# Where the tiles of a matmul stand in SBUF: the rooms in a fixed order, and one column of padding between the tiles of one of them

## The chip, the cores and the metric

The kernel runs on one core of one Trainium2 chip. The metric is the device time of one execution in microseconds (us); the time before is the median of three executions. Durations inside an execution come from one profiled execution of the same program.

## What is computed

A decoder trunk of two layers over 1024 tokens of width 1024, in float32. Each layer is a norm, one input projection, a retention group and a differential attention group, an output projection, and a gated feed-forward part:

```python
for l in range(DEPTH):
    u = rmsnorm(h, attn_norm[l])
    rq, rk, rv, rg, dq, dk, dv = split(u @ w_in[l])
    ret = silu(rg) * rmsnorm(retention_chunkwise(rq, rk, rv), ret_norm[l])
    dif = rmsnorm(diff_attention(dq, dk, dv, lam), diff_norm[l]) * (1.0 - lam_init)
    h = h + concat([ret, dif]) @ w_out[l]
    u = rmsnorm(h, ffn_norm[l])
    h = h + (silu(u @ w_gate[l]) * (u @ w_up[l])) @ w_down[l]
return rmsnorm(h, final_norm)
```

FFN_HIDDEN is 2816, that is 22 tiles of 128.

## The kernel before, in words

**A product in three matmuls.** A float32 product is made of operands of type float32r, which TensorE streams in one pass. Each operand is kept as two tiles: a rounded one (hi) and what the rounding lost (lo). `mm3` and `product` issue three matmuls for each piece of 128 in the contracted dimension: weights hi with data hi, weights hi with data lo, weights lo with data hi (L246 to L248 and L270 to L272). The weights are the stationary operand, 128x128, of which each matmul loads its own copy; the data is the moving operand, mostly 128x512. In a profile row such as `ps_mm<-u,w` the moving operand stands first after the arrow and the stationary one second. In `tm_pair` (L305 to L307) the roles are turned: tiles of `w` move, 256 columns at a time, and those of `u` are stationary.

**Rooms.** SBUF is shared out by tags, each with a fixed number of rooms that its tiles use in turn. `a4` (8 rooms), `wr` (3), `sp`, `ka`, `v`, `mx` (4 each) and `kb` (2) hold 1024 float32 in each partition, 4096 bytes; `w` (12), `t2` (5) and `acc` (2) hold 512, 2048 bytes; `nx`, `ny` (2 each), `z` and `m` (4 each) hold four numbers, 16 bytes, and each takes 32. `u` has 4 rooms of eight tiles with 512 columns, 16384 bytes. A tag's rooms are laid out, one behind the other, where the program first asks for that tag, so that the order in SBUF is the order of first use.

**Where they stand.** The constants end at byte 5472, which is 96 modulo 256. Every big room is a multiple of 256 bytes long, so that offsets modulo 256 change only at small pieces. In the kernel before the order is `a4`, `wr`, `sp`, `acc`, `kb` (all of them at 96 modulo 256), then `nx` and `ny` (4 x 32 = 128 bytes), then `u`, `t2`, `w`, `mx`, `ka`, `v` (all of them at 96 + 128 = 224 modulo 256). Tiles inside a room begin at multiples of 512 bytes, so the same holds for every tile and every 128-column slice of weights. Below, the *offset* of a matmul is the address of its moving tile less the address of the weights that are loaded while it runs, those of the matmul behind it, modulo 256. Before, it is 0 for data in `u`, `ka`, `v` with weights in `w` or `mx`, and 128 for data in `sp` with weights in `w`, for data in `u` with weights in `kb`, and for `ka` with `a4`.

**Who uses u.** `norm_half` writes the normed activations into two rooms of `u`, one for hi and one for lo, tile k of each for piece k (L421 to L432). `retention` writes the concatenated output there. In the feed-forward part seven data factors stand in rooms named by `TAGS7 = ["u", "u", "ka", "v", "u", "u", "sp"]`, four in `u`, one each in `ka`, `v` and `sp` (`views`); a factor in `u` uses one room, tiles 0 to 3 for hi and 4 to 7 for lo. The last six hidden tiles (`TAILS`) come through `layer`, and some of them also stand in `u`.

**Order of the work.** TensorE's order is written out by hand. In attention its projections are woven with score, transpose and value matmuls (`weave`); in the feed-forward part it runs long rows of 84 matmuls of 128x512 per hidden tile. ScalarE, VectorE and GpSimd make the hi and lo tiles, SyncE issues the DMAs.

Of the kernel before, what the change touches and what calls it, by code (L numbers as in the profile page):

```python
# [12 lines left out]
F32 = mybir.dt.float32  # L13
R32 = mybir.dt.float32r
# [4 lines left out]
P = 128  # L19
D = 1024  # L20
T = 1024
KT = D // P
NH = 2
HT = T // NH
# [5 lines left out]
FAST = 16  # L30
TAILS = [2, 4]
TAGS7 = ["u", "u", "ka", "v", "u", "u", "sp"]
RAWS = ["wr", "wr", "wr", "kb", "kb"]
EPS = 1e-6
NEG = -3.0e38
# [83 lines left out]
class Line:  # L119


    def __init__(self):
        self.n, self.tasks, self.products, self.w, self.made = -1, {}, [], {}, 0
# [23 lines left out]
class Trunk:  # L147
    def __init__(self, tc, ctx, a):
        self.tc, self.nc, self.a = tc, tc.nc, a
        pool = lambda name, **kw: ctx.enter_context(tc.tile_pool(name=name, bufs=1, **kw))  # L150
        self.sb = pool("sb")
        self.ps = pool("ps", space=bass.MemoryType.PSUM)
        self.dr = pool("dr", space=bass.MemoryType.DRAM)
        self.n = 0
        self.wi = 0
        self.consts()


    def t(self, tag, bufs, shape, dt=F32):
# [2 lines left out]

    def big(self, tag, dt=F32):
        return self.t(tag, {"a4": 8, "ka": 4, "kb": 2, "v": 4, "sp": 4, "mx": 4, "wr": 3}[tag], [P, 1024], dt)

    def tmp(self, dt=F32):
        return self.t("t2", 5, [P, 512], dt)
# [58 lines left out]
    def views(self, tag):  # L226

        if tag == "u":
            t = self.t("u", 4, [P, KT, HT], R32)
            return [(t[:, i], t[:, 4 + i]) for i in range(4)]  # L230
        t = [self.big(tag, R32) for _ in range(4)]
        c = [slice(0, 512), slice(512, 1024)]
        return [(t[i // 2][:, c[i % 2]], t[2 + i // 2][:, c[i % 2]]) for i in range(4)]
# [184 lines left out]
    def norm_half(self, h, hf, gcol, us, lag=11, gap=9, first=False, keep=False):  # L418
        nc = self.nc
        sl = slice(hf * HT, hf * HT + HT)  # L420
        parts = self.squares(h, sl, 0, True, first)  # L421
        yield lag
        y = yield from self.rsqrt_rows(parts, D, gap=gap)
        hi = self.t("u", 4, [P, KT, HT], R32)
        lo = self.t("u", 4, [P, KT, HT], R32)
        for k in range(KT):
            f = self.tmp()
            nc.vector.scalar_tensor_tensor(out=f, in0=h[k][:, sl], scalar=self.gains[:, gcol + k:gcol + k + 1],
                                           in1=y, op0=ALU.mult, op1=ALU.mult)
            nc.scalar.copy(hi[:, k], f)  # L430
            eng = nc.gpsimd if keep and k in (1, 4) else nc.vector
            eng.tensor_tensor(out=lo[:, k], in0=f, in1=hi[:, k].bitcast(F32), op=ALU.subtract)  # L432
        if keep:
            self.first_y = self.big("sp")[:, 0:HT]
            nc.scalar.copy(self.first_y, y)
        us[hf] = (hi, lo)
# [13 lines left out]
    def seven_second(self, h, gcol, b, keep, line):  # L450

        nc = self.nc
        v = nc.vector.tensor_tensor
        sl = slice(HT, T)
        parts = self.squares(h, sl, 0)
        yield 15
        y = yield from self.rsqrt_rows(parts, D, gap=9)
        own = self.t("u", 4, [P, KT, HT])
        t22, t12 = [own[:, i] for i in range(4)], [own[:, 4 + i] for i in range(4)]
        c = [slice(0, 512), slice(512, 1024)]  # L460
        b11, b21 = [keep[i // 2][:, c[i % 2]] for i in range(4)], [keep[2 + i // 2][:, c[i % 2]] for i in range(4)]
        b += [self.views(TAGS7[2]), self.views(TAGS7[3]), None, self.views(TAGS7[5]), None]
        two = [self.big("sp") for _ in range(2)]
        t2 = [two[i // 2][:, c[i % 2]] for i in range(4)]

        def norm(f, k):
            nc.vector.scalar_tensor_tensor(out=f, in0=h[k][:, sl], scalar=self.gains[:, gcol + k:gcol + k + 1],
                                           in1=y, op0=ALU.mult, op1=ALU.mult)

        def sub(out, x, z, q=None, i=0):  # L470
            v(out=out, in0=x, in1=z, op=ALU.subtract)
            if q is not None:
                nc.scalar.copy(b[q][i][0], out)

        def low(src, dst):
            v(out=dst[1], in0=src, in1=dst[0].bitcast(F32), op=ALU.subtract)
        r = range(4)
        ops = [lambda i=i: norm(t12[i], i) for i in r]
        ops += [lambda i=i: norm(t22[i], 4 + i) for i in r]
        for i in r:  # L480
            ops.append(lambda i=i: sub(b11[i], t12[i], b11[i]))
            ops.append(lambda i=i: sub(t2[i], t22[i], b11[i], 2, i))
        ops += [lambda i=i: low(t2[i], b[2][i]) for i in r]
        ops += [lambda i=i: self.part(b11[i], b[3][i], nc.vector) for i in r]

        def room(q):
            b[q] = self.views(TAGS7[q])
        ops += [lambda i=i: sub(b11[i], t22[i], t12[i]) for i in r]
        ops += [lambda i=i: self.part(t22[i], b[5][i], nc.vector) for i in r]
        ops.append(lambda: room(4))  # L490
        ops += [lambda i=i: self.part(b11[i], b[4][i], nc.vector) for i in r]
        ops += [lambda i=i: sub(b21[i], b21[i], t2[i]) for i in r]
        ops.append(lambda: room(6))
        ops += [lambda i=i: self.part(b21[i], b[6][i], nc.vector) for i in r]
        for i, op in enumerate(ops):
            line.later(line.n + (i // 3 if i < 21 else 7 + (i - 21) // 6 if i < 37 else 13), op)
# [558 lines left out]
    def right_factors(self, line, fast, m0):  # L1055
# [14 lines left out]
        def one(q, i):  # L1070
            if not b[q]:
                b[q] += self.views(TAGS7[q])
            self.part(stage[q, i - i % 2][:, 512 * (i % 2):512 * (i % 2) + 512], b[q][i],
# [9 lines left out]
    def down_fast(self, line, h, at, f0, b, m):  # L1083
# [3 lines left out]
        for e in range(2):  # L1087
            self.factors(line, at + 2 * e, {j: n0 + 2 * j + e for j in range(7)}, None,
                         [RAWS[(m + e) % 5], RAWS[(m + 2 + e) % 5]],
                         [n for n in range(n0, n0 + 14) if n % 3 == 0])  # L1090
# [25 lines left out]
    def layer(self, l, h, us, w_first, norm1, after):  # L1116
        nc, a = self.nc, self.a
# [5 lines left out]
                nc.sync.dma_start(src[k], h[k])  # L1123
        o_out, rq, rk = self.attention(l, us, w_first, norm1)
        x = self.retention_inputs(us, rq, rk, self.att_close(l))
        mix = [(self.t("u", 4, [P, KT, HT], R32), self.t("u", 4, [P, KT, HT], R32)) for _ in range(NH)]
        for hf in range(NH):
            for hd in range(4):
                s = o_out[hd][:, hf * HT:hf * HT + HT]
                hi, lo = mix[hf]  # L1130
# [6 lines left out]
        rhs = lambda k, hf: (mix[hf][0][:, k], mix[hf][1][:, k])  # L1137
        ws = [self.weight("w" if i < 3 else "kb") for i in range(4)]
        keep = [self.big("mx") for _ in range(4)]
        b = [self.views(tag) for tag in TAGS7[:2]]  # L1140
        self.two_halves(h, 4, ws, rhs, ["mm"], self.seven_first(h, 16 + 8 * l, b, keep))
# [5 lines left out]
        for ci, n in enumerate(TAILS):  # L1147
            acts = []
            for i in range(n):
                if n == 2 or i == 3:  # L1150
                    if n == 4 or i == 0:
                        room = self.t("u", 4, [P, KT, HT], R32).rearrange("p (a k) c -> p a (k c)", a=4)
                    j = 2 * (i % 2) if n == 2 else 0
                    acts.append((room[:, j], room[:, j + 1]))
                else:
                    tag = ["ka", "v", "sp"][i]
                    acts.append((self.big(tag, R32), self.big(tag, R32)))
                s = self.big("mx")
                nc.sync.dma_start(s, rest[t0 + i])
                for hf in range(NH):  # L1160
                    sl = slice(HT * hf, HT * hf + HT)
                    self.part(s[:, sl], [x[:, sl] for x in acts[i]], nc.vector if hf else nc.gpsimd)
            t0 += n
            rhs = lambda k, hf: (acts[k][0][:, hf * HT:hf * HT + HT], acts[k][1][:, hf * HT:hf * HT + HT])
            per = KT // n
            if ci + 1 < len(TAILS):
                for i in range(n):
                    w = self.weight()
                    for hf in range(NH):
                        for f in range(per * i, per * i + per):  # L1170
                            self.drain(self.down_group(h, w, f, hf, n, rhs, "t"))
            else:
                self.exp_ln_set()
                ws = [self.weight("w" if i else "mx") for i in range(4)]
                self.two_halves(h, n, ws, rhs, ["t", "mm"], *after(h))
                return h
# [95 lines left out]
```

## Time and profile before

| | us |
|---|---|
| median of three executions | 2296.06 (2294.91 to 2296.53) |
| the profiled execution: its own time | 2295.52 |
| its span, first to last instruction | 2293.7 |
| TensorE matmuls busy | 2258.2 (98%) |
| TensorE weight loads busy | 1895.4 (83%) |
| VectorE busy | 1396.5 (61%) |
| ScalarE busy | 1009.0 (44%) |
| GpSimd busy | 730.7 (32%) |

The profiled execution is 0.54 us under the median and 1.8 us over its own span. Matmuls overlap: the next one starts while the last results of the one before are still on the way. A row's duration is therefore longer than what the matmul costs in a stream, and the cost is read from the distance between two starts, called the *gap* below. The granted clock of the execution is 0.996 of full speed.

### The profile page before, as it was taken

To read this page: it belongs to the slowest core of one execution; us is meant where nothing else is said; L and a number is where in the kernel's file an instruction comes from. 1 tells how busy PE (TensorE), PEld (TensorE's weight loads), DVE (VectorE), ACT (ScalarE), POOL (GpSimd) and SP (SyncE) were. 2 spreads that over 40 slices of the span, in tenths; PEclk is the share of its full clock that TensorE was granted. 3 is DMA by queue.
4 is the path that set the end of the run, shared out by engine and by line. 5 is a ranking of instruction groups with operands and counts; after the bars stand their busy time and mean duration, and the time that the engine had idled before them with its cause. 6 is when DMAs were issued, how large, how long until landed. Compare 5 with 4: busy or idle time off the path is not lost.

```text
span 2293.7 us, 30632 instructions
## 1 busy us (share of the span) xinstructions
PE 2258.2 (98%) x11328; PEld 1895.4 (83%) x11328; DVE 1396.5 (61%) x2596; ACT 1009.0 (44%) x1905; POOL 730.7 (32%) x588
## 2 busy tenths in 40 slices
PE   7999999999999999999999999999999999999998
PEld 5888898887888888888888888988878888888887
DVE  8777612989544333895567775059884434359856
ACT  5666533445333333543256665234453333344332
POOL 3111212120455455336121112211205445544350
PEclk9999999999999999999999999999999999999999
DMA  4312131112333332652232222112123232346422
GB/s 162 81 47 65 39 97 40 55 56 63 135 106 99 108 106 91 231 183 93 68 108 56 55 66 81 58 38 74 48 96 120 91 116 91 109 150 200 158 65 74
DMA packets 74214, 216.58 MB, mean 94 GB/s; under 512 B 8016, under 2 KB 10064, under 8 KB 74064
## 3 DMA queue, kind: packets, MB, share of 16 engines
q1 hardware_dynamic: 74064, 214.62, 28.9%
q8 instruction: 89, 1.46, 0.3%
q14 instruction: 61, 0.50, 0.1%
HBM read 162.16 MB, written 44.04 MB: 90 GB/s over the span
## 4 chain that ended last, share of the span: by engine, by line
PE 84%; DVE 11%; ACT 2%; issue 1%; DMA 1%; POOL 0%; DVEq 0%; SPq 0%; ACTq 0%; POOLq 0%
PE ps_mm L246 8%; PE ps_mm L248 8%; PE ps_mm L247 8%; PE ps_mm L271 7%; PE ps_mm L270 7%; PE ps_mm L272 7%; PE ps_s L248 4%; PE ps_s L246 4%; PE ps_s L247 4%; PE ps_mm L307 3%; PE ps_mm L305 3%; PE ps_mm L306 3%; PE ps_t L248 2%; PE ps_t L247 2%; PE ps_t L246 2%; PE ps_s L556 1%
## 5 line engine op out<-in xcount | busy, mean ns | idle before, releaser
L223 POOL TENSOR_TENSOR w<-wr,w 128x512 fp32r<-128x512 f32 x262 | 367.4, 1416 | 446.8 <-ACT w L222 417.2
L263 POOL TENSOR_TENSOR w<-wr,w 128x512 fp32r<-128x512 f32 x140 | 184.9, 1327 | 578.6 <-ACT w L262 522.0
L270 PE MATMUL ps_mm<-u,w 128*128 128x512 f32 (+1 forms) x735 | 295.8, 403 | 0.0
L271 PE MATMUL ps_mm<-u,w 128*128 128x512 f32 (+1 forms) x735 | 287.1, 391 | 2.1 <-DVE u L432 2.1
L272 PE MATMUL ps_mm<-u,w 128*128 128x512 f32 (+1 forms) x735 | 287.3, 391 | 0.0
L222 ACT CAST w<-wr 128x512 fp32r<-128x512 f32 x312 | 187.4, 619 | 133.2 <-DVE wr L893 73.5
L246 PE MATMUL ps_mm<-u,w 128*128 128x512 f32 x432 | 168.6, 390 | 0.0
L247 PE MATMUL ps_mm<-u,w 128*128 128x512 f32 x432 | 168.3, 390 | 0.0
L248 PE MATMUL ps_mm<-u,w 128*128 128x512 f32 x432 | 168.3, 390 | 0.0
L272 PEld LDWEIGHTS ps_mm<-u,w 128*128 128x128 f32 x735 | 138.0, 188 | 30.2
L271 PEld LDWEIGHTS ps_mm<-u,w 128*128 128x128 f32 x735 | 138.3, 188 | 25.9 <-DVE u L432 2.8
L270 PEld LDWEIGHTS ps_mm<-u,w 128*128 128x128 f32 x735 | 138.2, 188 | 23.9
L942 ACT COPY t<-ps_mm 128x512 f32<-128x512 f32 x76 | 44.6, 586 | 243.4 <-PE ps_mm L248 243.1
L262 ACT CAST w<-wr 128x512 fp32r<-128x512 f32 x140 | 85.8, 619 | 128.3 <-PE ps_mm L271 39.0
L306 PE MATMUL ps_mm<-w,u 128*128 128x256 f32 x448 | 127.7, 285 | 0.7 <-POOL w L263 0.7
L305 PE MATMUL ps_mm<-w,u 128*128 128x256 f32 x448 | 128.4, 287 | 0.0
L307 PE MATMUL ps_mm<-w,u 128*128 128x256 f32 x448 | 127.5, 285 | 0.0
L223 POOL TENSOR_TENSOR w<-t,w 128x512 fp32r<-128x512 f32 x48 | 64.5, 1344 | 192.5 <-ACT w L222 192.5
L559 DVE CUSTOM_DVE_ANT_0 sp<-ps_s,wr 128x512 f32<-128x512 f32 (+2 forms) x192 | 102.9, 551 | 33.0 <-PE ps_s L557 32.1
L563 ACT ACTIVATE sp<-sp,m 128x256 f32<-128x256 f32 (+7 forms) x128 | 99.1, 775 | 50.8 <-DVE m L562 50.1
L851 DVE TENSOR_TENSOR a<-a,ps_mm 128x512 f32<-128x512 f32 (+1 forms) x148 | 98.6, 666 | 32.7 <-PE ps_mm L248 19.3
L891 DVE TENSOR_TENSOR t<-wr,wr 128x512 f32<-128x512 f32 x46 | 34.7, 755 | 116.5 <-DMA wr<-wts 116.1
(386 smaller groups left out, 5913.6 us busy)
## 6 DMA issues: line engine op xcount, KB each, us to landing
wr<-wts SPq DMA_DIRECT2D x190, 512.0 KB, 3.7
mx<-s_fast SPq DMA_DIRECT2D x56, 512.0 KB, 4.9
s_fast<-mx SPq DMA_DIRECT2D x48, 512.0 KB, 4.8
kb<-ka SPq DMA_DIRECT2D x64, 128.0 KB, 2.3
s_rest<-mx SPq DMA_DIRECT2D x12, 512.0 KB, 2.9
kb<-wts SPq DMA_DIRECT2D x12, 512.0 KB, 5.9
mx<-s_rest SPq DMA_DIRECT2D x12, 512.0 KB, 3.6
a<-xT SPq DMA_DIRECT2D x16, 256.0 KB, 5.4
```

The source lines that it names most:

```text
L222: nc.scalar.copy(h, src)
L223: (eng or nc.gpsimd).tensor_tensor(out=o, in0=src, in1=h.bitcast(F32), op=ALU.subtract)
L246: mm(ps, lhsT=wh[:, c], rhs=bh, start=first and i == 0, stop=False, skip_group_check=True)
L247: mm(ps, lhsT=wh[:, c], rhs=bl, start=False, stop=False, skip_group_check=True)
L248: mm(ps, lhsT=wl[:, c], rhs=bh, start=False, stop=i == 3, skip_group_check=True)
L263: nc.gpsimd.tensor_tensor(out=o, in0=raw[:, cols], in1=h.bitcast(F32), op=ALU.subtract)
L270: mm(out, lhsT=lh, rhs=rh, start=first, stop=False)
L271: mm(out, lhsT=lh, rhs=rl, start=False, stop=False)
L272: mm(out, lhsT=ll, rhs=rh, start=False, stop=last)
L305: mm(o, lhsT=uh, rhs=wh, start=k == 0, stop=False)
L306: mm(o, lhsT=uh, rhs=wl, start=False, stop=False)
L307: mm(o, lhsT=ul, rhs=wh, start=False, stop=k == KT - 1)
```

## The change

The order of the instructions on every engine, and what each waits for, is the same before and after; what differs is the addresses that they name.

1. `rooms()`, called at the end of `__init__`, asks for one tile of each tag in the order of the list `ROOMS`. With that, `nx` and `ny` come first, which moves `a4`, `wr`, `sp`, `acc` and `kb` from 96 to 224 modulo 256, where `t2`, `w`, `mx`, `ka` and `v` stand as before. `u` comes last of the big ones. The list holds no number, so no gap is put anywhere.
2. `room_u` gives the eight tiles of a room a pitch of 513 columns instead of 512, 2052 bytes. A room is now 16416 bytes long, 32 more than a multiple of 256. Tile t of room r (0 to 3) thus stands at 224 + 32 r + 4 t modulo 256, and its offset from weights in `w` is 32 r + 4 t: each of the values 0, 4, 8, ... 124 once.
3. In `layer` a tail tile in `u` can't be taken as 1024 columns in one piece any more, since its halves are no longer adjacent. `acts` keeps two halves for each of hi and lo instead.

```diff
+ROOMS = ["nx","ny","a4","wr","sp","acc","kb","t2","w","mx","ka","v","u"]
...
         self.consts()
+        self.rooms()
+
+    def rooms(self):
+
+        for i, x in enumerate(ROOMS):
+            if isinstance(x, int):
+                self.const(f"gap_{i}", [P, x // 4])
+            elif x == "u":
+                self.room_u()
+            elif x in ("w", "t2", "acc"):
+                self.t(x, {"w": 12, "t2": 5, "acc": 2}[x], [P, 512])
+            elif x in ("nx", "ny"):
+                self.t(x, 2, [P, 4])
+            elif x in ("z", "m"):
+                self.t(x, 4, [P, 4])
+            else:
+                self.big(x)
...
+    def room_u(self, dt=R32):
+
+        return self.t("u", 4, [P, KT, HT + 1], dt)[:, :, 0:HT]
...
         if tag == "u":
-            t = self.t("u", 4, [P, KT, HT], R32)
+            t = self.room_u()
...
-        hi = self.t("u", 4, [P, KT, HT], R32)
-        lo = self.t("u", 4, [P, KT, HT], R32)
+        hi = self.room_u()
+        lo = self.room_u()
...
-        own = self.t("u", 4, [P, KT, HT])
+        own = self.room_u(F32)
...
-        mix = [(self.t("u", 4, [P, KT, HT], R32), self.t("u", 4, [P, KT, HT], R32)) for _ in range(NH)]
+        mix = [(self.room_u(), self.room_u()) for _ in range(NH)]
...
-                        room = self.t("u", 4, [P, KT, HT], R32).rearrange("p (a k) c -> p a (k c)", a=4)
+                        room = self.room_u()
                     j = 2 * (i % 2) if n == 2 else 0
-                    acts.append((room[:, j], room[:, j + 1]))
+                    acts.append([[room[:, 2 * i + x] for x in range(2)] for i in (j, j + 1)])
...
-            rhs = lambda k, hf: (acts[k][0][:, hf * HT:hf * HT + HT], acts[k][1][:, hf * HT:hf * HT + HT])
+            rhs = lambda k, hf: (acts[k][0][hf], acts[k][1][hf])
```

More of the change, by code (lines that the diff above doesn't have):

```diff
@@ L1151, in layer @@
                     if n == 4 or i == 0:
-                        room = self.t("u", 4, [P, KT, HT], R32).rearrange("p (a k) c -> p a (k c)", a=4)
+                        room = self.room_u()
                     j = 2 * (i % 2) if n == 2 else 0
-                    acts.append((room[:, j], room[:, j + 1]))
+                    acts.append([[room[:, 2 * i + x] for x in range(2)] for i in (j, j + 1)])
                 else:
                     tag = ["ka", "v", "sp"][i]
-                    acts.append((self.big(tag, R32), self.big(tag, R32)))
+                    x = [self.big(tag, R32) for _ in range(2)]
+                    acts.append([[y[:, 0:HT], y[:, HT:T]] for y in x])
                 s = self.big("mx")
@@ L1161, in layer @@
                     sl = slice(HT * hf, HT * hf + HT)
-                    self.part(s[:, sl], [x[:, sl] for x in acts[i]], nc.vector if hf else nc.gpsimd)
+                    self.part(s[:, sl], [x[hf] for x in acts[i]], nc.vector if hf else nc.gpsimd)
             t0 += n
-            rhs = lambda k, hf: (acts[k][0][:, hf * HT:hf * HT + HT], acts[k][1][:, hf * HT:hf * HT + HT])
+            rhs = lambda k, hf: (acts[k][0][hf], acts[k][1][hf])
             per = KT // n
```

## The prediction

> **What bounds the kernel now.** I read the page first: who is busy, whether TensorE's clock is held back, and what the chain that ended last is made of.
>
> ```profile
> PE 2258.2 (98%) x11328; PEld 1895.4 (83%) x11328; DVE 1396.5 (61%) x2596; ACT 1009.0 (44%) x1905; POOL 730.7 (32%) x588
> PEclk9999999999999999999999999999999999999999
> PE 84%; DVE 11%; ACT 2%; issue 1%; DMA 1%; POOL 0%; DVEq 0%; SPq 0%; ACTq 0%; POOLq 0%
> ```
>
> TensorE is busy 98% of the span at full clock, and 84% of the chain that ended last is its matmuls. It never waits long, so the time is the sum of the gaps from one matmul's start to the next. The second view is therefore TensorE's timeline in the middle of the first feed-forward part, where a row of data in `u` gives way to data in `sp` and then to `u` again.
>
> ```profile
> 996.25 0.39 PE L246 MATMUL ps_s<-u,w 128*128 128x512 f32 x1
> ...
> 1001.47 0.39 PE L248 MATMUL ps_s<-u,w 128*128 128x512 f32 x1
> 1001.69 0.40 PE L246 MATMUL ps_mm<-sp,w 128*128 128x512 f32 x1
> 1001.93 0.39 PE L247 MATMUL ps_mm<-sp,w 128*128 128x512 f32 x1
> 1002.15 0.40 PE L248 MATMUL ps_mm<-sp,w 128*128 128x512 f32 x1
> 1002.39 0.39 PE L246 MATMUL ps_mm<-sp,w 128*128 128x512 f32 x1
> ...
> 1007.28 0.39 PE L246 MATMUL ps_mm<-u,w 128*128 128x512 f32 x1
> ```
>
> Between 996.25 and 1001.69 lie 24 matmuls on `u`: 5.44 / 24 = 226.7 ns each. Between 1001.69 and 1007.28 lie 24 on `sp`: 5.59 / 24 = 232.9 ns. Shape, type, weights and engine are the same; what differs is the offset, 0 for `u`, 128 for `sp`. So where a tile stands does cost time, 6.2 ns between these two. The third view is the groups with shapes kept apart, which say the same for the whole span.
>
> ```profile
> L246 PE MATMUL ps_mm<-u,w 128*128 128x512 f32 x432 | 168.6, 390 | 0.0
> L246 PE MATMUL ps_t<-u,w 128*128 128x512 f32 x264 | 102.9, 390 | 0.0
> L246 PE MATMUL ps_s<-u,w 128*128 128x512 f32 x248 | 96.5, 389 | 0.0
> L270 PE MATMUL ps_mm<-u,w 128*128 128x512 f32 x729 | 294.2, 404 | 0.0
> L272 PE MATMUL ps_mm<-u,w 128*128 128x512 f32 x729 | 285.6, 392 | 0.0
> L270 PE MATMUL ps_t<-u,w 128*128 128x512 f32 x73 | 28.6, 392 | 0.7 <-DVE a L851 0.6
> L246 PE MATMUL ps_mm<-sp,w 128*128 128x512 f32 x216 | 85.7, 397 | 0.5 <-DVE t L954 0.3
> L247 PE MATMUL ps_mm<-sp,w 128*128 128x512 f32 x216 | 85.1, 394 | 0.0
> L248 PE MATMUL ps_mm<-sp,w 128*128 128x512 f32 x216 | 85.3, 395 | 0.0
> L246 PE MATMUL ps_mm<-ka,w 128*128 128x512 f32 x216 | 84.1, 390 | 0.1
> L247 PE MATMUL ps_mm<-ka,w 128*128 128x512 f32 x216 | 84.0, 389 | 0.0
> L248 PE MATMUL ps_mm<-ka,w 128*128 128x512 f32 x216 | 84.0, 389 | 0.0
> L246 PE MATMUL ps_s<-v,w 128*128 128x512 f32 x216 | 84.0, 389 | 0.0
> L270 PE MATMUL ps_mm<-u,kb 128*128 128x512 f32 x32 | 12.7, 396 | 0.0
> L271 PE MATMUL ps_t<-sp,w 128*128 128x512 f32 x9 | 3.5, 387 | 0.0
> ```
>
> A mean of 389 goes with a gap of 226.7, so a gap is the mean less 162. `u`, `ka` and `v` in L246 to L248 have 389 or 390, `sp` 394 to 397, and `u` with weights in `kb`, the other pair at offset 128, 396. The shortest mean is 387, a gap of 225. Each of three lines has 432 + 264 + 248 = 944 matmuls of data in `u` on weights in `w` (L246 to L248) and 729 + 73 = 802 (L270 to L272): 5238 in all, 46% of the 11328.
>
> The fourth view is the timeline where such a row begins after another kind of matmul.
>
> ```profile
> 513.29 0.39 PE L248 MATMUL ps_mm<-u,w 128*128 128x512 f32 x1
> 513.52 0.40 PE L246 MATMUL ps_mm<-u,w 128*128 128x512 f32 x1
> 513.75 0.39 PE L247 MATMUL ps_mm<-u,w 128*128 128x512 f32 x1
> 513.98 0.40 PE L248 MATMUL ps_mm<-u,w 128*128 128x512 f32 x1
> 514.22 0.39 PE L246 MATMUL ps_mm<-u,w 128*128 128x512 f32 x1
> ...
> 515.13 0.39 PE L247 MATMUL ps_mm<-u,w 128*128 128x512 f32 x1
> ```
>
> From 513.29 to 514.22 four gaps take 0.93, 232 ns each, and from 514.22 to 515.13 four take 0.91, 227.5. At offset 0 the gap *settles* at 226.7 after some steps; until then it is that of `sp`, which does not settle. That is why L272 has 392 rather than 389: in attention its rows are cut by other matmuls. What a matmul needs without this loss is bounded by a plain float32 one:
>
> ```profile
> 393.78 1.03 PE L828 MATMUL ps_t<-v,mx 128*128 128x256 f32 x4
> L828 PE MATMUL ps_t<-v,mx 128*128 128x256 f32 x56 | 14.6, 383 | 0.6 <-DVE mx L783 0.6
> ```
>
> Both its operands are float32, each issued twice, and 256 columns take the streaming time of 512 of the other type. Four take 1.03 with a last one of 383 ns, so the gap is (1030 - 383) / 3 = 216 ns. A matmul at offset 0 thus loses 226.7 - 216 = 10.7 ns, one at 128 loses 17. The loss must come from the weights read while the data streams:
>
> ```profile
> 1000.11 0.19 PEld L246 LDWEIGHTS ps_s<-u,w 128*128 128x128 f32 x1
> 1000.34 0.19 PEld L247 LDWEIGHTS ps_s<-u,w 128*128 128x128 f32 x1
> ```
>
> A load starts with the matmul ahead of it and is over after 190 ns of 227, so TensorE does not wait for weights; the two streams get in each other's way.
>
> **The change part by part.**
>
> *`sp` goes from offset 128 to 0.* Same data, weights and order as `ka`, so it takes the gap of `ka`. The three groups of 216 give 85.7 + 85.1 + 85.3 = 256.1 against 84.1 + 84.0 + 84.0 = 252.1: -4.0 us. Smaller groups (other result tiles, the tails, `kb`, `ka` with `a4`), some 400 matmuls by the 6.2 ns, would give 2.5 if all settled; most stand in short rows that don't, so I take -1. Sum -5.0. Nothing hides this, since TensorE is the bound.
>
> *`u` goes from offset 0 to 0, 4, ... 124.* No row of the trace has an offset between 0 and 128, so this is bounded on both sides: 216 (plain float32, no loss) and 232.9 (`sp`, offset 128). Against 226.7 that is -10.7 to +6.2 ns, by 5238: -56 to +32 us. I take -3.0 ns, a gap of 224, near the shortest mean of the type (387, a gap of 225): -15.7 us. The reason for the sign: both offsets that the trace shows are multiples of 128 bytes, and both lose; at 0 the streams even begin in step. Three of four tiles would now begin 4, 8 or 12 bytes out of step with a group of four numbers, and the hi and lo tiles of one piece stand 16 bytes or whole multiples of 32 apart, so that no two neighbours meet the weights alike. Such spreading helps if the loss is the two streams meeting in the same place at the same time. It is the weakest step of this text.
>
> *`u` as weights.* `tm_pair` has 1344 + 192 matmuls with `u` stationary, 256 columns:
>
> ```profile
> L305 PE MATMUL ps_mm<-w,u 128*128 128x256 f32 x448 | 128.4, 287 | 0.0
> L602 PE MATMUL ps_o<-a,v 128*128 128x256 f32 x160 | 39.4, 282 | 0.0
> ```
>
> 285 to 287 at offset 0, 282 at offset 128 (`v` with `a4`): between -5 and +5 ns by 1536 is 8 us either way; I take 0.
>
> *Writing and addressing `u`.* Tiles at odd multiples of 4 bytes are written by ScalarE, VectorE and GpSimd, and no row shows what that costs. The nearest is the plain write:
>
> ```profile
> L238 DVE TENSOR_TENSOR u<-mx,u 128x512 fp32r<-128x512 f32 x86 | 80.4, 959 | 21.6 <-ACT u L237 21.6
> ```
>
> and TensorE's waits name that helper once:
>
> ```profile
> PE ps_t L246 <- ACT u L237: 1.1, 2, 0.6
> ```
>
> Even a tenth more on these writes is 8 us on an engine that is idle 39% of the span, and TensorE waits 1.1 us in all for tiles of `u` made there: 0, at most +1. The tails' split halves are the same instructions.
>
> Sum: -5.0 - 15.7 = -20.7. On the profiled execution's 2295.52 that is 2274.8; the median stands 0.54 higher, so 2275.4, rounded to **2276**.
>
> **The rivals.**
>
> *The row never settles (slower).* If 226.7 needs neighbours that meet the weights alike, `u` loses it and runs like the start at 513.29 or like `sp`, 232 ns. The 2832 matmuls of L246 to L248 lose 5.3 ns, 15.0 us; the 2406 of L270 to L272, of which many are unsettled now (392 against 389), lose some 2.7, 6.5 us. `ka`, `v` and `sp` settle anew behind `u`: four steps of 5 ns, as at 513.29, twice in each of 216 x 3 / 12 = 54 rows, 2.2 us. Less the 5.0 of `sp`: +18.7, 2315. It decides from an average gap on `u` of about 228.5. For it: three of three cases not settled lie between 231 and 233, and none under 224. Against it: only two offsets are known. [...]
>
> *Only `sp` gains.* If an offset under 128 counts as 0, `u` stays at 226.7: -5, 2291.
>
> *Nothing changes.* If the 6.2 ns belong to something else in `sp`, such as the result bank, the time stays at 2296. Against it: the pair `u` with `kb` shows them as well. [...]
>
> **How the numbers follow.** Two executions can tell about 0.2% apart, 4.6 us. Forecast 0.52, never settles 0.33, only `sp` 0.08 (half of it beyond the bound), nothing 0.07. Faster 0.52 + 0.04 = 0.56, same 0.04 + 0.07 = 0.11, slower 0.33. The forecast's own range is 2254 (a gap of 219.7 on `u`, two thirds of the way to 216: -7.0 ns by 5238 and -5) to 2291 (no gain on `u`). The whole range reaches up into the slower case, to 2314, just under its 2315; it leaves out about half of that case and the far end of the gains.
>
> **What would show it.** In the changed profile, between 600 and 1100 us: `sp` in L246 to L248 at 389 instead of 395, and `u` below 389 with fewer rows of 0.40 in the timeline. `u` at 393 or more there means the row does not settle, and I am wrong with the sign; `u` at 389 with `sp` at 389 means only `sp` gained; `sp` still at 395 means the offset is not the cause. VectorE's writes to `u` above 959 with TensorE waiting for them would be a cost that I put at nothing.

## The result and the profile after

The changed kernel takes 2306.13 us (median of four, 2305.28 to 2307.01) against 2296.28 us (four, 2294.91 to 2296.53) beside it: a ratio of 1.0043 (95% interval 1.0029 to 1.0056). It is slower by 9.9 us, where 2276 was forecast. The profiled execution took 2306.9 us; its span is 2305.1 us, 11.4 more than before.

The page after has the same picture as before: the number of matmuls (11328) and the granted clock (0.997 against 0.996) are unchanged, and the chain that ended last is still mostly TensorE's matmuls, 86% of it against 84%.

```profile
PE 2272.1 (99%) x11328; PEld 1896.5 (82%) x11328; DVE 1393.8 (60%) x2596; ACT 1009.2 (44%) x1905; POOL 725.2 (31%) x588
PEclk9999999999999999999999999999999999999999
PE 86%; DVE 10%; issue 2%; ACT 1%; DMA 1%; POOL 0%; DVEq 0%; SPq 0%; ACTq 0%; POOLq 0%
```

TensorE's matmuls are busy 13.9 us longer (2258.2 before). VectorE and GpSimd do less; the weight loads and ScalarE grow by 1.1 and 0.2 us. The waits of TensorE hold nothing of that size either: the three longest were 5.7, 3.3 and 3.7 us before, and are now (columns: total us, times, longest):

```profile
PE ps_mm L311 <- DMA a<-xT: 5.7, 2, 5.5
PE ps_s L402 <- DVE acc L437: 4.0, 3, 2.8
PE ps_s L418 <- DVE ny L414: 3.8, 5, 1.3
```

So the time went into the matmuls' own gaps. Lines stand 22 further down than before: L246 to L248 are now L268 to L270, L270 to L272 are L292 to L294, L305 to L307 are L327 to L329. The groups with shapes kept apart:

```profile
L292 PE MATMUL ps_mm<-u,w 128*128 128x512 f32 x729 | 296.2, 406 | 0.0
L294 PE MATMUL ps_mm<-u,w 128*128 128x512 f32 x729 | 287.4, 394 | 0.0
L268 PE MATMUL ps_mm<-u,w 128*128 128x512 f32 x432 | 170.2, 394 | 0.1
L268 PE MATMUL ps_t<-u,w 128*128 128x512 f32 x264 | 104.4, 396 | 0.0
L268 PE MATMUL ps_s<-u,w 128*128 128x512 f32 x248 | 98.0, 395 | 0.0
L268 PE MATMUL ps_mm<-sp,w 128*128 128x512 f32 x216 | 84.8, 393 | 0.6 <-DVE t L976 0.6
L269 PE MATMUL ps_mm<-sp,w 128*128 128x512 f32 x216 | 84.3, 390 | 0.0
L270 PE MATMUL ps_mm<-sp,w 128*128 128x512 f32 x216 | 84.1, 389 | 0.0
L268 PE MATMUL ps_mm<-ka,w 128*128 128x512 f32 x216 | 84.4, 391 | 0.0
L327 PE MATMUL ps_mm<-w,u 128*128 128x256 f32 x448 | 128.1, 286 | 0.0
L328 PE MATMUL ps_mm<-mx,u 128*128 128x256 f32 x64 | 18.0, 282 | 0.0
```

`sp` has come down from 394 to 397 to 389 to 393, nearly what `ka` has. `u` in L268 has gone up from 389 or 390 to 394, 395 and 396. `tm_pair`, where `u` is the weights, has hardly moved (L327: 286, 287 before). The timeline at the same place of the first feed-forward part, rows of `u` and then of `sp`:

```profile
1000.81 0.40 PE L268 MATMUL ps_s<-u,w 128*128 128x512 f32 x1
...
1003.86 0.39 PE L269 MATMUL ps_s<-u,w 128*128 128x512 f32 x1
...
1006.43 0.39 PE L268 MATMUL ps_mm<-sp,w 128*128 128x512 f32 x1
...
1011.65 0.39 PE L270 MATMUL ps_mm<-sp,w 128*128 128x512 f32 x1
```

13 gaps on `u` take 3.05 us, 234.6 ns each; 23 on `sp` take 5.22, 227.0 each. The two have changed places.

Summed over the span from the starts of all matmuls (moving tile on weights; where a mean is given, gaps over 300 ns are left out of it):

| | count | before, us | after, us | difference |
|---|---|---|---|---|
| `u` on `w`, 512 columns | 5286 | 1226.9 | 1245.5 | +18.6 |
| `sp` on `w`, 512 columns | 774 | 180.6 | 176.8 | -3.8 |
| `mx` on `u`, 256 columns | 192 | 27.6 | 25.7 | -1.9 |
| `w` on `u`, 256 columns | 1344 | 164.7 | 163.1 | -1.6 |
| all the rest | | | | +0.4 |
| sum | | | | +11.7 |

The mean gap on `u` rose from 228.0 to 232.0 ns, that on `sp` fell from 232.6 to 227.9. The sums hold the waits as well. On `u` the 4.0 ns make 20.7 us over the 5150 gaps up to 300 ns, and the long gaps give 2.1 back. Of the -1.9 for `mx` on `u` only 0.2 lies in gaps up to 300 ns; the rest are waits, and e1b_order below has 25.7 as well, with `u` at offset 0.

### The profile page after: what moved, and what is told of

Its sections match the earlier page's. It is cut to its first block, busy times and chain, and to the rows that moved or that the text cites. A ratio compares the mean times of both kernels' runs of the same rounds, so it can differ in the third digit from the quotient of the medians.

```text
span 2305.1 us, 30632 instructions
## 1 busy us (share of the span) xinstructions
PE 2272.1 (99%) x11328; PEld 1896.5 (82%) x11328; DVE 1393.8 (60%) x2596; ACT 1009.2 (44%) x1905; POOL 725.2 (31%) x588
## 4 chain that ended last, share of the span: by engine, by line
PE 86%; DVE 10%; issue 2%; ACT 1%; DMA 1%; POOL 0%; DVEq 0%; SPq 0%; ACTq 0%; POOLq 0%
PE ps_mm L268 8%; PE ps_mm L269 8%; PE ps_mm L270 8%; PE ps_mm L293 7%; PE ps_mm L292 7%; PE ps_mm L294 7%; PE ps_s L268 4%; PE ps_s L270 4%; PE ps_s L269 4%; PE ps_mm L327 3%; PE ps_mm L329 3%; PE ps_mm L328 3%; PE ps_t L268 2%; PE ps_t L270 2%; PE ps_t L269 2%
## 5 line engine op out<-in xcount | busy, mean ns | idle before, releaser
L292 PE MATMUL ps_mm<-u,w 128*128 128x512 f32 (+1 forms) x735 | 297.9, 405 | 0.0
L294 PE MATMUL ps_mm<-u,w 128*128 128x512 f32 (+1 forms) x735 | 289.0, 393 | 0.0
L268 PE MATMUL ps_mm<-u,w 128*128 128x512 f32 x432 | 170.2, 394 | 0.1
L270 PE MATMUL ps_mm<-u,w 128*128 128x512 f32 x432 | 169.4, 392 | 0.0
L294 PEld LDWEIGHTS ps_mm<-u,w 128*128 128x128 f32 x735 | 138.4, 188 | 31.8
L292 PEld LDWEIGHTS ps_mm<-u,w 128*128 128x128 f32 x735 | 138.6, 189 | 25.2
L327 PE MATMUL ps_mm<-w,u 128*128 128x256 f32 x448 | 128.1, 286 | 0.0
L329 PE MATMUL ps_mm<-w,u 128*128 128x256 f32 x448 | 126.9, 283 | 0.0
L268 PE MATMUL ps_t<-u,w 128*128 128x512 f32 x264 | 104.4, 396 | 0.0
```

Source lines behind the costliest of these rows:

```text
L268: mm(ps, lhsT=wh[:, c], rhs=bh, start=first and i == 0, stop=False, skip_group_check=True)
L270: mm(ps, lhsT=wl[:, c], rhs=bh, start=False, stop=i == 3, skip_group_check=True)
L292: mm(out, lhsT=lh, rhs=rh, start=first, stop=False)
L294: mm(out, lhsT=ll, rhs=rh, start=False, stop=last)
L327: mm(o, lhsT=uh, rhs=wh, start=k == 0, stop=False)
L329: mm(o, lhsT=ul, rhs=wh, start=False, stop=k == KT - 1)
```

## The experiments

Both parts of the change did something, with opposite signs. Open was why `u` lost. The theories, as the expectations call them:

- **A**: what costs is that neighbouring matmuls have different offsets; any one offset for all settles (the prediction's rival).
- **B**: each offset has a gap of its own, 0 a low one, 128 a high one; the 4-byte steps spread `u` over dear ones.
- **C**: what costs is that tiles don't begin on a group of 16 bytes.
- **D** (from the second batch on): the absolute place of the tiles counts, not the difference.
- **E** (likewise): the distance between the two streams counts, whichever of them is ahead.

Each edit below is shown against the changed kernel, those of e6_const252 and e7_const192 against e4_const4. An integer in `ROOMS` is a gap of so many bytes. Single executions are compared with the 2296.1 us (median of 13) or 2296.2 us (one) of the kernel before on the same chip. The gap of a row is worked out as in the prediction: distance between starts, or group mean less 162. A mean over the span is that of all gaps up to 300 ns on `u` with weights in `w`, as in the table above.

**e1_order and e1b_order: the order of the rooms alone**, without the column of padding; all big tiles at 224 modulo 256, all offsets 0.

```diff
-        return self.t("u", 4, [P, KT, HT + 1], dt)[:, :, 0:HT]
+        return self.t("u", 4, [P, KT, HT], dt)
```

> The order of the rooms alone: the tiles of u keep a pitch of 512 columns, so that all data on weights in w, sp too, is at offset 0. All three theories expect the same here: the gap on sp falls from 232.9 to 226.7 ns, that on u stays near 227, and the time is 4 to 5 us under before, 2291 to 2292. If instead the time is near 2306, the order and not the column of padding is what costs.

Measured: 2290.54 us (median of ten, 2288.47 to 2293.26) against 2296.08 (13): ratio 0.9978 (0.9969 to 0.9988). The groups of the profiled execution:

```profile
L268 PE MATMUL ps_mm<-u,w 128*128 128x512 f32 x432 | 168.5, 390 | 0.0
L268 PE MATMUL ps_mm<-sp,w 128*128 128x512 f32 x216 | 84.8, 393 | 0.7 <-DVE t L976 0.6
L269 PE MATMUL ps_mm<-sp,w 128*128 128x512 f32 x216 | 84.1, 389 | 0.0
L270 PE MATMUL ps_mm<-sp,w 128*128 128x512 f32 x216 | 84.1, 389 | 0.0
L328 PE MATMUL ps_mm<-w,u 128*128 128x256 f32 x448 | 127.6, 285 | 0.3 <-POOL w L285 0.3
```

`u` is where it was before the change (390), `sp` has the gap of `ka`; its sum falls by 4.2 us. So the order alone gains 5.5 us, and the column of padding costs 2306.1 - 2290.5 = 15.6 us. The same file was run again on another chip, beside the last experiment:

> The order alone once more, on the same chip as the kernel with a4 64 bytes short, to compare the two. It should stand 4 to 7 us under before, as it did (ratio 0.9978); all theories expect the same.

Measured: 2290.52 us (seven, 2288.17 to 2292.26) against 2296.24 (ten): 0.9973 (0.9962 to 0.9984). The gain repeats.

**e2_gap64: one offset for all of `u`, but 64**. As e1_order, with 64 bytes left free ahead of `u`.

```diff
-ROOMS = ["nx","ny","a4","wr","sp","acc","kb","t2","w","mx","ka","v","u"]
+ROOMS = ["nx","ny","a4","wr","sp","acc","kb","t2","w","mx","ka","v",64,"u"]
...
-        return self.t("u", 4, [P, KT, HT + 1], dt)[:, :, 0:HT]
+        return self.t("u", 4, [P, KT, HT], dt)
```

> As the order alone, but 64 bytes of nothing ahead of u, so that every tile of u is at offset 64 from the weights, all alike. Theory A (the gap settles at 226.7 ns whenever one matmul meets the weights as the one before it did, whatever the offset): u at 226.7, 2291. Theory B (each offset has a gap of its own, and the spread ones are dearer than 0): u near the 231.5 that tiles at offset 64 have in the changed kernel, 2291 + 5238 x 4.5 ns = 2315. Theory C (a tile costs more that begins inside a group of 16 bytes): 64 is a multiple of 16, so u at 226.7, 2291.

Measured: 2297.43 us, 6.9 more than with the order alone. The groups:

```profile
L268 PE MATMUL ps_mm<-u,w 128*128 128x512 f32 x432 | 170.9, 396 | 0.5 <-DVE a L873 0.4
L269 PE MATMUL ps_mm<-u,w 128*128 128x512 f32 x432 | 168.5, 390 | 0.0
L270 PE MATMUL ps_mm<-u,w 128*128 128x512 f32 x432 | 169.5, 392 | 0.0
L328 PE MATMUL ps_mm<-w,u 128*128 128x256 f32 x448 | 125.4, 280 | 0.0
```

All neighbours are alike, and the rows do settle, in a pattern of 226, 229 and 232 ns in turn, 229.0 on average. The mean over the span is 229.8, and `u` loses 10.0 us against the kernel before. Theory A falls in the form "alike is enough". And 64 is a multiple of 16: C does not explain this loss. With the roles turned (offset 192 there) 256 columns fall from 285 to 280: 121.7 to 117.0 ns a matmul, which gives back 6.7 us. So there is an offset that is better than 0, for the other shape.

**e3_step16: steps of 16 bytes instead of 4**, so that every tile begins on a group of 16 bytes; offsets 0, 16, ... 240. To make room, the scratch area of dynamic DMAs is halved.

```diff
-        return self.t("u", 4, [P, KT, HT + 1], dt)[:, :, 0:HT]
+        return self.t("u", 4, [P, KT, HT + 4], dt)[:, :, 0:HT]
...
-    nc = bacc.Bacc("TRN2", target_bir_lowering=False, num_devices=1, dynamic_dma_scratch_size=1024)
+    nc = bacc.Bacc("TRN2", target_bir_lowering=False, num_devices=1, dynamic_dma_scratch_size=512)
```

> The tiles of u with a pitch of 516 columns, so that each lies 16 bytes further off (0, 16, 32 and so on to 240), room for it taken from the unused scratch of the GpSimd DMAs. Theory A (neighbours must meet the weights alike): no row settles, u at 231 to 233 ns, 2306 to 2315. Theory B (each offset its own gap): the mean over multiples of 16, 231.8 by the changed kernel's tiles, 2310. Theory C (begin inside a group of 16 bytes): all tiles begin on such a group, so u at 226.7 and 2291.

Measured: 2307.79 us, `u` +19.2 us, a mean gap of 231.9: no better than steps of 4. One of the groups:

```profile
L269 PE MATMUL ps_mm<-u,w 128*128 128x512 f32 x432 | 170.1, 394 | 0.0
```

C falls. Here the tiles at offset 0 have a mean of 232.0, where e1_order has 227.6: the offset is the same and only the neighbours' differ, so that in a mixed row the neighbours do count. Of theory A this much stays. This kernel has each offset twice, with 256 bytes between the two; their means agree within 0.3 ns, so counting modulo 256 is right.

**e4_const4: all of `u` at offset 4.** A room is taken 64 columns longer and viewed from column 1; scratch is cut to 64 and a gap put in front, so that it fits and the other rooms stand alike among themselves, at 96 modulo 256.

```diff
-ROOMS = ["nx","ny","a4","wr","sp","acc","kb","t2","w","mx","ka","v","u"]
+ROOMS = [64,"nx","ny","a4","wr","sp","acc","kb","t2","w","mx","ka","v","u"]
...
-        return self.t("u", 4, [P, KT, HT + 1], dt)[:, :, 0:HT]
+        t = self.t("u", 4, [P, KT * HT + 64], dt)[:, 1:1 + KT * HT]
+        return t.rearrange("p (k c) -> p k c", k=KT)
...
-    nc = bacc.Bacc("TRN2", target_bir_lowering=False, num_devices=1, dynamic_dma_scratch_size=1024)
+    nc = bacc.Bacc("TRN2", target_bir_lowering=False, num_devices=1, dynamic_dma_scratch_size=64)
```

> Every tile of u at offset 4 from the weights, all alike: rooms of u lengthened to a multiple of 256 bytes and its tiles begun one column in, pitch 512; the scratch of the GpSimd DMAs is cut for it and all rooms stand 128 bytes lower modulo 256. Theory A (alike is enough): u settles at 226.7 ns, 2291. Theory B (each offset its own gap): u near the 233 that offset 4 has in the changed kernel, 2320. Theory C (begin inside a group of 16 bytes): u above 226.7, at 230 to 234, 2306 to 2325; it can't be told from B here, only by the kernels at 64 and with steps of 16.

Measured: 2331.6 us, the slowest of all. Its timeline where a row of `u` begins:

```profile
1005.11 0.40 PE L269 MATMUL ps_mm<-u,w 128*128 128x512 f32 x1
...
1012.25 0.40 PE L269 MATMUL ps_s<-u,w 128*128 128x512 f32 x1
```

30 gaps take 7.14 us, 238.0 ns each, from the first one on; the mean over the span is 237.5, and `u` loses 43.6 us. One offset for all can thus be worse than the mixture (232.0). A falls again, B stands.

**e5_base0: another absolute place.** As e1_order, with all rooms 32 bytes further on, at 0 modulo 256.

```diff
-ROOMS = ["nx","ny","a4","wr","sp","acc","kb","t2","w","mx","ka","v","u"]
+ROOMS = [32,"nx","ny","a4","wr","sp","acc","kb","t2","w","mx","ka","v","u"]
...
-        return self.t("u", 4, [P, KT, HT + 1], dt)[:, :, 0:HT]
+        return self.t("u", 4, [P, KT, HT], dt)
```

> The order alone with 32 bytes of nothing ahead of all rooms, so that every tile of data and of weights begins at 0 modulo 256 instead of 224, with all offsets between them still 0. Theory B (the gap goes by the offset between data and weights, each value having its own): nothing changes against the order alone, u at 227.6 ns, 2290.5. Rival D (the place of a tile itself counts, for instance whether it begins on a multiple of 64): u, ka, v and sp all move together, away from 226.7 by some ns, up or down: with some 7600 such matmuls, 2 ns are 15 us, 2275 or 2306.

Measured: 2288.41 us, inside the range of e1b_order on the same chip (2288.17 to 2292.26). The same group as in e1_order:

```profile
L268 PE MATMUL ps_mm<-u,w 128*128 128x512 f32 x432 | 168.5, 390 | 0.0
```

`u` is at 227.6 ns in both; in e9_a4 below, where `u` and `w` stand at 160 modulo 256, it is at 227.7. The absolute place does not show. D falls.

**e6_const252 and e7_const192: the other side of 0.** As e4_const4, from column 63 (offset 252, which is 4 bytes short) and from column 48 (offset 192, 64 short).

```diff
-        t = self.t("u", 4, [P, KT * HT + 64], dt)[:, 1:1 + KT * HT]
+        t = self.t("u", 4, [P, KT * HT + 64], dt)[:, 63:63 + KT * HT]
```

> Every tile of u 4 bytes short of the weights modulo 256 (offset 252) instead of 4 bytes past them, built like the kernel with all tiles at offset 4, which took 2331.6 with a gap of 237.5 on u. Theory B with a residue (what counts is the offset modulo 16: in the changed kernel tiles at 12 modulo 16 have the shortest gaps, 228.4 to 230.4, those at 4 modulo 16 the longest, 233 to 237): u at 229 or less, under 2300. Rival E (what counts is how far the two are apart, either way): u at 237 again, 2330.

Measured: 2301.61 us. Its timeline in a row of `u`:

```profile
1009.83 0.39 PE L269 MATMUL ps_mm<-u,w 128*128 128x512 f32 x1
...
1012.59 0.39 PE L269 MATMUL ps_mm<-u,w 128*128 128x512 f32 x1
```

12 gaps in 2.76 us: 230.0 ns, where 4 bytes to the other side gave 238. E falls: it counts which stream is ahead. The pair also speaks against C: no tile of either begins on a group of 16 bytes, yet one costs 2.4 ns and the other 9.9 over the 227.6 of e1_order, and offset 64, a multiple of 16, costs 2.2.

```diff
-        t = self.t("u", 4, [P, KT * HT + 64], dt)[:, 1:1 + KT * HT]
+        t = self.t("u", 4, [P, KT * HT + 64], dt)[:, 48:48 + KT * HT]
```

> Every tile of u at offset 192, 64 bytes short of the weights, instead of 64 past them, which gave 229.7 ns on u and 117 on the 256-column matmuls with u stationary (121.8 at offset 0). In those the moving tile stood at 192 past the weights. If the offset's sign counts (theory B), a moving u at 192 gains as they did, some 5 ns: u at 222, and the 256-column ones go the other way; 5286 x 5.6 ns less than the order alone, about 2265. If only the distance counts (rival E): u at 229.7, 2297. If 512 columns do not follow 256: anywhere between 226 and 237, 2290 to 2330.

Measured: 2312.53 us. Its timeline in a row of `u`:

```profile
1000.15 0.39 PE L269 MATMUL ps_mm<-u,w 128*128 128x512 f32 x1
...
1007.15 0.39 PE L269 MATMUL ps_s<-u,w 128*128 128x512 f32 x1
```

30 gaps in 7.00 us: 233.3 ns, `u` +26.8 us. The hope behind this run was that 192, the best offset for 256 columns, would be good for 512 as well; it was a miss. The offset that suits one shape does not suit the other.

**e8_rooms32: the rooms' 32 bytes without the 4-byte steps.** In the change a room is 32 bytes longer than a multiple of 256; here only that is left, and the rooms stand at offsets 0, 32, 64 and 96.

```diff
-        return self.t("u", 4, [P, KT, HT + 1], dt)[:, :, 0:HT]
+        t = self.t("u", 4, [P, KT * HT + 8], dt)[:, 0:0 + KT * HT]
+        return t.rearrange("p (k c) -> p k c", k=KT)
```

> The rooms of u 32 bytes longer each and a pitch of 512 inside them, so that the four rooms stand at offsets 0, 32, 64 and 96, all tiles of a room alike. The changed kernel without its steps of 4 bytes. If the steps inside a room are what costs, u falls from 232.2 towards 228, 2295. If the rooms' own offsets cost as much (theory B): the tiles at 64 as in the kernel with all at 64 (229.7), those at 0 at 227 to 229, and the mean of u at 229 to 231, 2297 to 2305.

Measured: 2305.09 us, `u` +15.8 us, a mean gap of 231.1. The timeline where a row in the room at 32 is followed, after `sp`, by one in the room at 0:

```profile
1000.04 0.40 PE L269 MATMUL ps_s<-u,w 128*128 128x512 f32 x1
...
1004.25 0.40 PE L269 MATMUL ps_s<-u,w 128*128 128x512 f32 x1
...
1010.41 0.39 PE L269 MATMUL ps_mm<-u,w 128*128 128x512 f32 x1
...
1013.81 0.39 PE L269 MATMUL ps_mm<-u,w 128*128 128x512 f32 x1
```

18 gaps in 4.21 us are 233.9 ns, 15 in 3.40 are 226.7. Over the span the rooms have 228.5 (0), 232.1 (32), 230.3 (64) and 233.9 (96). From the ninth gap at one offset on, the rows have 226.8, 233.3, 229.0 and 234.0. So each room goes to a level of its own inside one execution, and the one at 64 to that of e2_gap64. The four levels average 230.8, 4.0 above the first, enough for the 3.5 ns that `u` loses here against e1_order (231.1 against 227.6). Of the 15.6 us that the padding costs, 2305.1 - 2290.5 = 14.6 come from the rooms' displacement; the 4-byte steps add about 1, less than two executions can tell apart.

**e9_a4: a use of what e2 showed.** Only `a4` is moved, 64 bytes short of the others, so that in the value matmuls of attention (`a` on `v`, 256 columns) the offset is 192; `u`, `sp`, `ka` and `v` on `w` stay at 0.

```diff
-ROOMS = ["nx","ny","a4","wr","sp","acc","kb","t2","w","mx","ka","v","u"]
+ROOMS = ["a4","nx","wr","sp","acc","kb","t2","w","mx","ka","v","u","ny"]
...
-        return self.t("u", 4, [P, KT, HT + 1], dt)[:, :, 0:HT]
+        return self.t("u", 4, [P, KT, HT], dt)
```

> The order alone, but nx stands between a4 and the rest, so that a4 lies 64 bytes short of all other rooms; u, ka, v and sp stay at offset 0 from w. Theory B, carried to a pair of tiles that no kernel so far has moved: the 480 value matmuls of attention (256 columns, a4 moving, v stationary) go to offset 192, the one at which 256 columns took 113 to 117 ns when u was 64 past the weights; they fall from 121 to about 115, 480 x 6 ns = 2.9 us. The score matmuls (ka and kb moving, a4 stationary) go to offset 64, 229 to 232 as before. Sum: 2 to 3 us under the order alone, 2287 to 2288. Rival: the 117 belonged to u and not to the offset, or the next weights set it; then the value matmuls stay at 120 to 121 and the time is that of the order alone.

Measured: 2287.45 us (five, 2286.97 to 2289.8) against 2296.24 (ten): 0.9964 (0.9949 to 0.9978), the best of all. The value matmuls of e9_a4, and then of e1_order:

```profile
L623 PE MATMUL ps_o<-a,v 128*128 128x256 f32 x160 | 39.2, 282 | 0.0
L624 PE MATMUL ps_o<-a,v 128*128 128x256 f32 x160 | 38.5, 279 | 0.0
```

```profile
L623 PE MATMUL ps_o<-a,v 128*128 128x256 f32 x160 | 40.0, 285 | 0.0
L624 PE MATMUL ps_o<-a,v 128*128 128x256 f32 x160 | 39.7, 283 | 0.0
```

All of them together take 56.9 us instead of 58.5 (58.8 in e1b_order), a mean gap of 117.6 ns where about 115 was expected, against 121.0. That is 1.9 of the 3.1 us by which the medians on this chip differ (2290.52 in e1b_order); the two kernels' ranges overlap, so that the rest is not shown to belong to the edit.

The gaps of 512 columns where a whole row has one offset, in ns. The first line is the mean over the span where all of `u` has that offset (128: `sp` before the change); the second counts gaps from the ninth at one offset on (32 and 96 in e8_rooms32, 128 in the kernel before):

| offset | 0 | 64 | 252 | 128 | 32 | 192 | 96 | 4 |
|---|---|---|---|---|---|---|---|---|
| over the span | 227.6 | 229.8 | 230.0 | 232.6 | | 233.3 | | 237.5 |
| settled | 226.8 | 229.0 | 230.1 | 233.1 | 233.3 | 233.3 | 234.0 | 237.7 |

No offset that was tried has a shorter gap than 0. Theory B holds for rows of one offset, and the ladder has no simple order by distance or by alignment. Nor does the offset modulo 16 decide it, which e6_const252 had asked: 0, 32 and 64 share that and differ. In mixed rows the neighbours come on top (e3_step16). The sizes that theory B took from the mixed rows of the changed kernel missed accordingly: 2315 was expected at 64 and 2320 at 4, and 2297.4 and 2331.6 came.

## Why the prediction was wrong

*`u` from offset 0 to 0, 4, ... 124: -3.0 ns, -15.7 us.* This is the step that failed, with its sign. Measured: 228.0 to 232.0 ns, +4.0, and +18.6 us. The prediction argued that 0 and 128 both lose against 216 ns, that "at 0 the streams even begin in step", and that spreading helps. But 216 is the gap of another type, whose matmuls leave two records each (56 for the 28 calls of L828), where those of float32r leave one (L246, L247 and L248 in turn). Nothing in the trace said that 512 columns of float32r had an offset with a shorter gap than 0; the seven others measured in rows of one offset all have longer ones. That the whole distance from 216 to the measured gaps is a loss to the weights read meanwhile was the author's estimate; the runs show the part that goes with the offset, 226.8 to 237.7 ns. The 224 that the prediction took stood beside the group of nine with a mean of 387. Those nine stand at offset 128, and the matmuls just ahead of and just behind each of them, at the same offset in the kernel before, are these:

```profile
L270 PE MATMUL ps_t<-sp,w 128*128 128x512 f32 x9 | 3.6, 395 | 0.0
L272 PE MATMUL ps_t<-sp,w 128*128 128x512 f32 x9 | 3.6, 398 | 0.0
```

The three average 393, a gap of 231: a short gap between two long ones, not a cheaper matmul. In e1_order, at offset 0, all three groups have 389. Of the rows known, only settled ones at offset 0 had 226.7; those at 128 and those not settled, quoted at 513.29, had 231 to 233. The prediction's own range for this step (-56 to +32 us) held the result; no whole row supported the value taken from it. (Its sum of 2275.4 rounds to 2275, not 2276; nothing hangs on that.)

*`sp` from 128 to 0: -5.0 us.* Right in kind; measured -3.8 in the change and -4.2 in e1_order. The main groups were expected at 252.1 us and came to 84.8 + 84.3 + 84.1 = 253.2. In e1_order, where `u` and `sp` both stand at 0, they come to 253.0, so the missing 1 us is not the price of the new offsets of `u`; most of it lies in the first line, 393 against 390 for `ka`. The pairs `u` on `kb` and `ka` and `kb` on `a4` give 1.1 in e1_order, near the 1 taken for the smaller groups. e1_order shows the step alone, with 5.5 us by the medians.

*`u` as weights: 0 (8 us either way).* Measured -1.6 for `w` on `u` and -0.2 in the gaps of `mx` on `u`, inside the bounds. e2_gap64 shows that the bound was a real possibility: with one good offset it is -6.7 for `w` alone.

*Writing `u` at odd addresses: 0, at most +1.* Right. VectorE's plain write after the change:

```profile
L260 DVE TENSOR_TENSOR u<-mx,u 128x512 fp32r<-128x512 f32 x86 | 80.1, 955 | 21.0 <-ACT u L259 21.0
```

955 ns against 959, and of the same helper ScalarE 618 in both (L237, now L259), GpSimd 1352 against 1461: tiles at odd multiples of 4 bytes cost the engines that write them nothing here.

*The rival "the row never settles": 2315.* It had the sign, and for `u` the size: +21.5 expected, +18.6 measured, 232 ns expected, 232.0 measured. It expected 2.2 us from neighbours that settle anew: `ka` and `v` on `w` rose by 0.7 and 0.3 ns, some 0.8 us together, and `sp` stood 0.9 ns above e1_order, 0.7 us. The 1.6 us that `w` on `u` gained it put at nothing, as the forecast did. Its mechanism is only half right. Alike neighbours are not enough: offset 4 for all is worse than the mixture, and e8_rooms32, with one offset in each room, loses nearly as much as the change. But neighbours do shift a tile in a mixture: in the changed kernel the tiles at 0 have 229.3 (227.6 in e1_order) and those at 4 have 233.0 (237.5 in e4_const4). The runs give no rule for that shift. That the level of the mixture was near the rival's 232, which it took from rows not settled, is luck as far as the runs show.

*The other rivals* fall: the offset matters (`sp`, 232.6 to 227.9 ns), and offsets under 128 do not count as 0 (64 has 229.8, 4 has 237.5).

What stays open is why the levels are as they are. The runs show the levels at eight of the 64 offsets, not the reason; the others were seen only in mixed rows. Nor is it settled that the weights loaded meanwhile are the ones that count, since nearly all these rows take their own and the next weights from `w`. One place speaks for it: 92 matmuls of `u` on `w`, each ahead of one with weights in `a4`, have 232.7 ns before (next weights at 128) and 229.0 in e1_order (0), their own weights at 0 in both; in e9_a4 (64) it is 229.1.

## What to carry to other kernels

In a stream of matmuls that is TensorE-bound, the place of the moving tile against that of the weights was worth up to 5% of a matmul here (226.8 to 237.7 ns), so bring all big rooms to one residue modulo 256 first (5.5 us here, e1_order), before trying anything finer, and watch that small pieces between them don't displace them (with the 128 bytes of `nx` and `ny` between them `sp` had 232.6 ns on `w`, and 227.9 after). A padding that spreads tiles over many offsets mixed cheap and dear ones here (a mean of 232.0, where 0 alone has 227.6); without a measured offset that is cheaper, expect the mean of the known ones, not better than the best. Test one constant offset at a time, for each shape by itself (192 has 233.3 ns at 512 columns, where 0 has 227.6, and 117.0 at 256, where 0 has 121.7), and read the gap, not the row's duration.

## What the runs showed that had not been expected

- The sign of the offset counts: 4 bytes ahead costs 237.5 ns, 4 bytes short 230.0. At 256 columns, `w` on `u`, the ladder is another: 121.7 ns at 0 (e1_order), 119.8 at 64 (e7_const192), 117.0 at 192 (e2_gap64).
- At some offsets settled rows sit on a grid. At offset 0 most gaps are 227 or 226 ns, two to one (2807 and 1400 of 5149 in e1_order), 226.67 on average; at 192 they are 233 and 234, two to one (2592 and 1325 of 5157), 233.33. At 256 columns it is 120, or 113 and 114 two to one, 113.33. These are 34, 35, 18 and 17 times 6.667 ns. Other offsets do not sit on it: 64 goes through 226, 229 and 232 (229.0), 252 averages 230.1 and 4 averages 237.7. What the step is, and why some offsets keep to it, no run here shows.
